# Attention scores from high and low parts in a one-core decoder trunk

## The chip, the cores and the metric

The kernel runs on one core of one Trainium2 chip. Its time is the device time of one launch in microseconds (us). The host lays the weights out in the order of their loads beforehand; that is not part of the time.

## The reference

One residual layer with stick-breaking attention, between two RMS norms; 256 rows, width 4096, 32 heads of 128.

```python
h = x + attn_branch(rms_norm(x, norm_attn), w_in_attn, w_out_attn)
out = rms_norm(h, final_norm)

# attn_branch: one product with a 4096 x 16384 matrix, the heads, one with a 4096 x 4096 matrix
q, k, v, g = split(xn @ w_in, 4)
z = q @ k.T / sqrt(128)                       # the scores of a head, 256 x 256, causal
log_fail = where(causal, log_sigmoid(-z), 0)
suffix = reverse_cumsum(log_fail) - log_fail
a = where(causal, exp(log_sigmoid(z) + suffix), 0)
branch = ((a @ v) * silu(g)) @ w_out
```

All data is float32.

## The kernel before

**The two large products.** Weights come in tiles `raw` of 128 rows by 2 x 512 numbers. Each is taken apart into a high part `wh` (a cast by ScalarE, ACT, to the rounded type fp32r) and a low part `wl` (a subtraction on VectorE, DVE). The activations have been split in the same way (`sh`, `sl`, later `oh`, `ol`). `mm3` then makes one product as three matmuls: high by high, high by low, low by high, each of 512 columns. "Product" below means these three matmuls on TensorE (PE). The work goes in units of two heads' width: 16 for the first matrix (units 0 to 15), 8 for the second. A unit has 16 steps; most units do part of their steps with 7 products instead of 8, for which DVE makes sums of tiles (`raw<-raw,raw`) after a DMA issued by GpSimd (POOL) has added one block of a tile onto another in place.

**The heads.** While unit u+1 multiplies, the two heads of unit u pass through `head(u, i)`. It transposes q and k on PE into the PSUM bank `tr`, copies them to SBUF with ACT (`qkT`), and makes the scores `z`, which hold 384 columns: the 128 x 128 block of late keys and late queries, and the 128 x 256 block of early keys. Then come the logarithm of the failure probability (`f`, four ACT operations and one on DVE), its high and low part (`fh`, `fl`), the suffix sums as matmuls with a triangle of ones (`neg_tri`, fp32r operands, called the scan here), the weights `a`, and the product with v (`o`). The scores and the product with v are matmuls of plain fp32 operands. In lines 848 to 852:

```python
        def scores():
            kw = dict(stop=False, skip_group_check=True)
            nc.tensor.matmul(z[:, 0:P], qk[:, 1, P:S], qk[:, 0, P:S], start=True, **kw)
            nc.tensor.matmul(z[:, P:BW], qk[:, 1, 0:P], qk[:, 0, :], start=False, **kw)
```

followed by a bf16 matmul with `ident_b` that adds a large negative number where a key does not come before its query (`off`).

**What sets the order.** No order is written out. The class `Plan` plays the kernel through while it is built: each step asks for an engine with an estimated cost, the step with the earliest due time goes next, and the instructions are recorded in that order, which each engine then keeps. Rings model the buffers: `gh` has 4 places of SBUF that all stages of the heads share, `att` is the one PSUM bank of the heads, `wl` has 5 places, `raw` has 7. `nc.take` waits for a place, `nc.give` hands it back. Products always go in the same sequence; work of the heads is put between them when it is ready in the plan. All instructions are recorded by one helper, so the profile gives nearly every one the line L132, and one goes by the names of tiles.

Of the kernel before, what the change touches and what calls it, by code (L numbers as in the profile page):

```python
# [10 lines left out]
F32 = mybir.dt.float32  # L11
F32R = mybir.dt.float32r
# [7 lines left out]
P = 128  # L20
S = 256
# [31 lines left out]
ROWS = 4  # L53
# [47 lines left out]
def vector_ns(n):  # L101
    return 67 + 1.0417 * n


def scalar_ns(n):
    return 98 + n / 1.2


def tensor_ns(n):
    return 0.4167 * n + 8.5 if n > 128 else 109.0  # L110
# [138 lines left out]
def kernel(  # L249
# [10 lines left out]
    nc = Plan(tc)  # L260
# [3 lines left out]
    wp = ctx.enter_context(tc.tile_pool(name="weights", bufs=1))  # L264
# [10 lines left out]
    def minus(out_, full, part):  # L275
        nc.vector.tensor_tensor(out=out_, in0=full, in1=part.bitcast(F32), op=ALU.subtract)
# [34 lines left out]
    for g, (n, k) in enumerate(order):  # L311
        p = parts[n]
        b = p["u"], p["prods"][k][0]
# [12 lines left out]
    def soon(c=4.0):  # L326
        return nc.here + 1e3 * c


    def dve(emit, n, key=None, more=0, **kw):  # L330
        n = n if isinstance(n, tuple) else (n,)
        cost = sum(vector_ns(m) for m in n) + 122 * (len(n) - 1) + more
        return nc.work("vector", cost, emit, soon() if key is None else key, **kw)

    def act(emit, n, key=None, **kw):
        n = n if isinstance(n, tuple) else (n,)
        cost = sum(scalar_ns(m) for m in n) + 100 * (len(n) - 1)
        return nc.work("scalar", cost, emit, soon() if key is None else key, **kw)


    FULL_P, FULL_S = (P,) * 2, (W,) * 2
# [3 lines left out]
    def ten(emit, *n):  # L345
        def others():
            nonlocal since_others
            since_others = 0
            emit()

        return nc.work("tensor", 40 + sum(tensor_ns(m) for m in n), others, nc.here - 1e4, wait=400)
# [469 lines left out]
    BW = 3 * P  # L821
    not_before = off.broadcast_to([P, 2, P])

    def head(u, i):
        yield nc.take("att", "gh", sooner=True)
        tr = att.tile([P, 2, S], F32, tag="att", name=f"tr{u}_{i}")

        def turn():
            for k in range(2):
                for t in range(NT):  # L830
                    c = k * CW + i * P
                    nc.tensor.transpose(tr[:, k, t * P : (t + 1) * P], st["qk", u][:, t, c : c + P], ident)

        yield ten(turn, P, P, P, P)
        if i == HG - 1:
            nc.give("one")
        qk = wp.tile([P, 2, S], F32, tag="gh", name=f"qkT{u}_{i}", bufs=ROWS)
        yield act(lambda: nc.scalar.copy(qk, tr), 2 * S)
        nc.give("att")
        yield nc.take("att", sooner=True)  # L840
        bank = att.tile([P, W], F32, tag="att", name=f"z{u}_{i}")
        z, gT = bank[:, 0:BW], bank[:, BW:W]

        def turned(to, t):
            nc.tensor.transpose(to, st["gv", u][:, t, i * P : (i + 1) * P], ident)

        def scores():
            kw = dict(stop=False, skip_group_check=True)
            nc.tensor.matmul(z[:, 0:P], qk[:, 1, P:S], qk[:, 0, P:S], start=True, **kw)
            nc.tensor.matmul(z[:, P:BW], qk[:, 1, 0:P], qk[:, 0, :], start=False, **kw)  # L850
            diagonal = z[:, 0 : 2 * P].rearrange("p (a b) -> p a b", a=2)
            nc.tensor.matmul(diagonal, ident_b, not_before, start=False, **kw)

        yield ten(scores, *FULL_P, *FULL_S, 2 * P)
        nc.give("gh")
        yield nc.take("gh", sooner=True)

        f = wp.tile([P, BW], F32, tag="gh", name=f"f{u}_{i}", bufs=ROWS)

        def soft():  # L860
            nc.scalar.activation(f, z, AF.Abs, scale=scale)
            nc.scalar.activation(f, f, AF.Exp, scale=-1.0)
            nc.scalar.activation(f, f, AF.Ln, bias=1.0)
            nc.scalar.activation(f, f, AF.Copy, scale=1.0 / scale)

        yield act(soft, (BW,) * 4)
        yield dve(
            lambda: nc.vector.scalar_tensor_tensor(out=f, in0=z, scalar=0.0, in1=f, op0=ALU.max, op1=ALU.add), BW
        )
        yield nc.take("gh", "gh", sooner=True)  # L870
        fh, fl = (wp.tile([P, BW], F32R, tag="gh", name=f"f{k}{u}_{i}", bufs=ROWS) for k in "hl")
        yield act(lambda: nc.scalar.copy(fh, f), BW)
        yield dve(lambda: minus(fl, f, fh), BW)
        nc.give("gh")

        if i == 0:
            yield nc.until(("gate", u))

        def scan():
            kw = dict(start=False, skip_group_check=True)  # L880
            nc.tensor.matmul(z, neg_tri, fh, stop=False, **kw)
            nc.tensor.matmul(z, neg_tri, fl, stop=False, **kw)
            nc.tensor.matmul(z[:, 2 * P : BW], neg_one, fh[:, 0:P], stop=False, **kw)
            nc.tensor.matmul(z[:, 2 * P : BW], neg_one, fl[:, 0:P], stop=True, **kw)
            turned(gT, 0)

        yield ten(scan, BW, BW, P, P, P)
        nc.give("gh", "gh")
        if i == 0:
            yield nc.take("gh", sooner=True)  # L890
            st["o", u] = wp.tile([P, 4, P], F32, tag="gh", name=f"gated{u}", bufs=ROWS)
        gated = st["o", u][:, 2 * i : 2 * i + 2, :].rearrange("p a b -> p (a b)")
        yield nc.take("gh", sooner=True)
        a = wp.tile([P, BW], F32, tag="gh", name=f"a{u}_{i}", bufs=ROWS)


        def weights_of():
            nc.scalar.activation(a, z, AF.Relu, scale=-scale)
            nc.scalar.activation(a, a, AF.Exp, scale=-1.0)

        yield act(weights_of, (BW, BW))
        yield act(lambda: nc.scalar.copy(gated[:, 0:P], gT), P)
        nc.give("att")
        yield nc.take("att", sooner=True)
        bank2 = att.tile([P, BW], F32, tag="att", name=f"o{u}_{i}")
        o, gT2 = bank2[:, 0:S], bank2[:, S:BW]
        v = lambda t: st["gv", u][:, t, CW + i * P : CW + (i + 1) * P]

        def out_of_head():
            kw = dict(skip_group_check=True)  # L910
            nc.tensor.matmul(o, v(0), a[:, P:BW], start=True, stop=False, **kw)
            nc.tensor.matmul(o[:, P:S], v(1), a[:, 0:P], start=False, stop=True, **kw)
            turned(gT2, 1)

        yield ten(out_of_head, *FULL_P, *FULL_S, P)
        nc.give("gh")
        if i == HG - 1:
            nc.give("two")
        yield act(lambda: nc.scalar.copy(gated[:, P:S], gT2), P)
        yield dve(lambda: nc.vector.tensor_tensor(out=gated, in0=o, in1=gated, op=ALU.mult), S)  # L920
        nc.give("att")
# [3 lines left out]
    def heads(u):  # L925
        nc.start(gate(u))
        yield nc.until(("qk", u))
        for i in range(HG):
            yield from head(u, i)

        nc.tell(("heads", u))
        if u < NS - 1:
            spill[u] = dp.tile([P, 4, P], F32, name=f"spill{u}")
            yield moved(
                "gpsimd", lambda: nc.gpsimd.dma_start(spill[u], st["o", u]), [4 * P], soon(),
                after=lambda: (nc.give("gh"), nc.tell(("spilled", u))),
            )
# [396 lines left out]
```

## Time and profile before

| | before |
|---|---|
| median of three timed runs | 1700.52 us (1699.19 to 1701.03) |
| profiled execution, its own time | 1698.9 us |
| span in that profile | 1697.1 us |
| granted TensorE clock, mean | 0.997 |
| PE busy | 1680.2 us, 99% |
| DVE busy | 1602.0 us, 94% |
| ACT busy | 1206.7 us, 71% |
| POOL busy | 324.9 us, 19% |
| HBM | 242 GB/s over the span |

Busy time is the union of the spans of an engine's instructions. Matmuls are pipelined: one of 512 columns lasts 0.38 us in the profile and yet the next starts 0.22 us after it, so the spacing tells the cost and not the length. DVE's instructions overlap a little in the same way. "PEld" is the weight load of a matmul, which has a row of its own. In the timeline, "x4" after a row means four instructions in a row that were merged.

### The profile page before, as it was taken

What the parts mean: (1) busy time and instruction counts of PE and PEld (TensorE: products, weight loads), DVE (VectorE), ACT (ScalarE), POOL (GpSimd) and SP (SyncE); (2) the same over time, 40 slices, a digit from 0 to 9 for tenths busy, and PEclk for the clock granted to TensorE, in tenths of its full rate; (3) what the DMA queues carried; (4) which work ended last, traced back from release to release, by engine and by line L of the source; (5) the groups of instructions that cost most, each with busy time, mean ns of one, the idle gap of its engine ahead of it and who ended that gap; (6) DMA issues with size and microseconds to landing.
All of it is one profiled execution on the core that took longest, in us unless ns stands there. A gap on an engine that the chain in (4) does not pass through costs nothing.

```text
span 1697.1 us, 25128 instructions
## 1 busy us (share of the span) xinstructions
PE 1680.2 (99%) x7776; PEld 1417.4 (84%) x7776; DVE 1602.0 (94%) x2025; ACT 1206.7 (71%) x1665; POOL 324.9 (19%) x400
## 2 busy tenths in 40 slices
PE   9999999999999999999999999999999999999997
PEld 7888888888888888888888888888888888888885
DVE  8899999999999999999999999999999978999997
ACT  8986767676767676767676767676868775656654
POOL 0012222121222222222212121212122111212110
PEclk9999999999999999999999999999999999999998
DMA  9978888878787878797978797979797978888895
GB/s 343 332 197 247 232 247 222 252 217 253 215 256 212 256 212 266 199 272 196 276 201 269 198 268 196 272 198 269 204 264 210 300 230 266 245 245 256 246 304 185
DMA packets 248438, 412.77 MB, mean 243 GB/s; under 512 B 28016, under 2 KB 72560, under 8 KB 248304
## 3 DMA queue, kind: packets, MB, share of 16 engines
q1 hardware_dynamic: 194544, 354.24, 62.7%
q0 software_dynamic: 53472, 56.65, 20.0%
q8 instruction: 61, 1.00, 0.2%
q14 instruction: 73, 0.60, 0.1%
q10 hardware_dynamic: 288, 0.28, 0.1%
HBM read 402.93 MB, written 8.13 MB: 242 GB/s over the span
## 4 chain that ended last, share of the span: by engine, by line
PE 94%; DVE 3%; DMA 1%; issue 1%; ACT 1%; SPq 0%; DVEq 0%; ACTq 0%
PE acc L132 89%; PE z L132 3%; PE o L132 1%; DVE wl L132 1%; PE tr L132 1%; DVE h L132 1%; DVE raw L132 0%; ACT wh L132 0%; DMA raw<-in_w_out_dram 0%; DMA raw<-in_w_in_dram 0%; DMA xres<-in_x_dram 0%; SPq L132 0%; ACT sq L132 0%; DVE scalars L132 0%; DVE qk_sb L132 0%
## 5 line engine op out<-in xcount | busy, mean ns | idle before, releaser
L132 ACT CAST wh<-raw 128x1024 fp32r<-128x1024 f32 (+1 forms) x989 | 919.3, 970 | 385.5 <-DVE raw L132 160.9
L132 DVE TENSOR_TENSOR wl<-raw,wh 128x1024 fp32r<-128x1024 f32 (+1 forms) x815 | 975.7, 1220 | 49.3 <-ACT wh L132 23.9
L132 PE MATMUL acc<-wh,sh 128*128 128x512 f32 x2048 | 771.9, 389 | 0.1
L132 PE MATMUL acc<-wh,sl 128*128 128x512 f32 x1898 | 727.1, 383 | 1.8 <-DVE sl L132 1.8
L132 PE MATMUL acc<-wl,sh 128*128 128x512 f32 x1748 | 668.9, 383 | 0.1
L132 PEld LDWEIGHTS acc<-wh,sh 128*128 128x128 f32 x2048 | 384.0, 188 | 77.9 <-DVE qk_sb L132 4.9
L132 POOL DMA_DIRECT2D raw<-in_w_in_dram x300 | 258.3, 947 | 972.2 <-DMA raw<-in_w_in_dram 375.1
L132 PEld LDWEIGHTS acc<-wh,sl 128*128 128x128 f32 x1898 | 356.0, 188 | 66.3 <-DVE sl L132 2.4
L132 PEld LDWEIGHTS acc<-wl,sh 128*128 128x128 f32 x1748 | 328.4, 188 | 55.6 <-DVE wl L132 0.4
L132 DVE TENSOR_TENSOR raw<-raw,raw 128x512 f32<-128x512 f32 x348 | 238.3, 688 | 15.3 <-DMA raw<-in_w_in_dram 11.7
L132 PE MATMUL acc<-wh,oh 128*128 128x512 f32 x512 | 192.4, 383 | 0.0
L132 PE MATMUL acc<-wh,ol 128*128 128x512 f32 x488 | 186.7, 383 | 0.0
L132 PE MATMUL acc<-wl,oh 128*128 128x512 f32 x464 | 177.6, 383 | 1.4 <-DVE wl L132 1.4
L132 DVE TENSOR_TENSOR wh<-raw,wh 128x512 fp32r<-128x512 f32 x174 | 119.7, 688 | 3.3 <-ACT wh L132 2.7
L132 DVE TENSOR_TENSOR raw<-raw 128x512 f32<-128x512 f32 x174 | 119.4, 686 | 0.0
L132 PEld LDWEIGHTS acc<-wh,oh 128*128 128x128 f32 x512 | 96.1, 188 | 17.3
L132 PEld LDWEIGHTS acc<-wh,ol 128*128 128x128 f32 x488 | 91.5, 188 | 16.1
L132 PEld LDWEIGHTS acc<-wl,oh 128*128 128x128 f32 x464 | 87.1, 188 | 17.6 <-DVE wl L132 2.2
L132 POOL DMA_DIRECT2D raw<-in_w_out_dram x48 | 41.5, 984 | 173.8 <-DMA raw<-in_w_out_dram 85.2
L132 ACT ACTIVATE f<-f 128x384 f32<-128x384 f32 x96 | 50.5, 526 | 3.0
L132 POOL DMA_DIRECT2D p<-spill x27 | 17.0, 676 | 89.9 <-DVE ol L132 32.0
L132 DVE SCALAR_TENSOR_TENSOR gv_sb<-acc,scalars,gv_sb 128x512 f32<-128x512 f32 x45 | 33.5, 745 | 0.0
(86 smaller groups left out, 765.7 us busy)
## 6 DMA issues: line engine op xcount, KB each, us to landing
raw<-in_w_in_dram SPq DMA_DIRECT2D x1024, 256.0 KB, 4.5
raw<-in_w_out_dram SPq DMA_DIRECT2D x256, 256.0 KB, 4.5
raw<-in_w_in_dram POOLq DMA_DIRECT2D x300, 128.0 KB, 5.2
p<-spill POOLq DMA_DIRECT2D x27, 256.0 KB, 4.6
raw<-in_w_out_dram POOLq DMA_DIRECT2D x48, 128.0 KB, 5.4
xr<-in_x_dram SPq DMA_DIRECT2D x16, 256.0 KB, 5.3
xres<-in_x_dram SPq DMA_DIRECT2D x16, 256.0 KB, 5.5
out_dram<-h SPq DMA_DIRECT2D x16, 256.0 KB, 2.8
```

The lines of the kernel that those rows point to most:

```text
L132: return self.tc.keep_in_program_order(getattr(self.engine, name)(*args, **kw))
```

## The change

`head` now makes two tiles out of the transposed q and k: `qkh`, which ACT writes rounded to fp32r, and `qkl`, which DVE writes as the difference between the PSUM bank and `qkh`. So the head takes a second place of the ring `gh` from here to the scores, and gives the PSUM bank back only after the subtraction. The two fp32 matmuls of the scores become six matmuls of fp32r operands, three for each block. The cost that the plan is told for the scores changes too.

```diff
-        qk = wp.tile([P, 2, S], F32, tag="gh", name=f"qkT{u}_{i}", bufs=ROWS)
+        yield nc.take("gh", sooner=True)
+        qk, ql = (wp.tile([P, 2, S], F32R, tag="gh", name=f"qk{k}{u}_{i}", bufs=ROWS) for k in "hl")
         yield act(lambda: nc.scalar.copy(qk, tr), 2 * S)
+        yield dve(lambda: minus(ql, tr, qk), 2 * S)
         nc.give("att")
...
-            nc.tensor.matmul(z[:, 0:P], qk[:, 1, P:S], qk[:, 0, P:S], start=True, **kw)
-            nc.tensor.matmul(z[:, P:BW], qk[:, 1, 0:P], qk[:, 0, :], start=False, **kw)
+            for keys, queries, to in ((slice(P, S), slice(P, S), z[:, 0:P]), (slice(0, P), slice(0, S), z[:, P:BW])):
+                for a, b in ((qk, qk), (qk, ql), (ql, qk)):
+                    first_ = a is b and keys.start == P
+                    nc.tensor.matmul(to, a[:, 1, keys], b[:, 0, queries], start=first_, **kw)
...
-        yield ten(scores, *FULL_P, *FULL_S, 2 * P)
-        nc.give("gh")
+        yield ten(scores, BW, BW, BW, 2 * P)
+        nc.give("gh", "gh")
```

Since the plan decides the order, instructions move. Three places of unit 5 show it; its first head is `5_0`, its second `5_1`, the number behind a tile's name is its buffer, and the number in `wl300` counts the split tiles.

On PE, the scores of head 5_0, before:

```order
L132 MATMUL acc6_5_5138<-wl293_5054,sh0_79 128x4x16x8
L132 MATMUL acc6_5_5138<-wh293_5017,sl0_80 128x4x16x8
L132 MATMUL z5_0_5148<-qkT5_0_5136 128x128
L132 MATMUL z5_0_5148<-qkT5_0_5136 128x256
L132 LDWEIGHTS ident_b_140
L132 MATMUL z5_0_5148<-off_139,ident_b_140 128x256
L132 MATMUL acc6_3_5157<-wh293_5017,sh0_79 128x4x32x4
```

and now:

```order
L132 MATMUL acc6_3_5214<-wh293_5077,sl0_80 128x4x16x8
L132 MATMUL z5_0_5221<-qkh5_0_5196 128x128
L132 MATMUL z5_0_5221<-qkl5_0_5197,qkh5_0_5196 128x128
L132 MATMUL z5_0_5221<-qkh5_0_5196,qkl5_0_5197 128x128
L132 MATMUL z5_0_5221<-qkh5_0_5196 128x256
L132 MATMUL z5_0_5221<-qkl5_0_5197,qkh5_0_5196 128x256
L132 MATMUL z5_0_5221<-qkh5_0_5196,qkl5_0_5197 128x256
L132 LDWEIGHTS ident_b_140
L132 MATMUL z5_0_5221<-off_139,ident_b_140 128x256
L132 MATMUL acc6_1_5233<-wh294_5106,sh1_86 128x4x32x4
```

Six matmuls stand where two stood (the profile shows each of the two fp32 ones as two). Counted in the whole order, the scores of a unit's first head stand 5 products after its transposes where 3 stood between; for the second head it is 5 in both, and its transposes and scores stand one product earlier than they did. The scan of the first head stays at its product and that of the second moves one product earlier; the product with v stays where it was. Only in unit 15, whose heads run beside the first products with the second matrix, is the shift larger: its first scores stand 14 products after the transposes instead of 2, and its last product with v 15 products later than before.

On DVE, the stretch behind the last addition that makes q, k, v and g of unit 5 (`gv_sb5<-acc5_3`), before:

```order
L132 SCALAR_TENSOR_TENSOR gv_sb5_5027<-acc5_3_4356,scalars_77,gv_sb5_5027 128x512
L132 TENSOR_TENSOR wl297_5144<-raw97_0_4990,wh297_5068 128x1024
L132 TENSOR_TENSOR raw98_0_5019<-raw98_0_5019,raw98_1_5006 128x2x256
L132 TENSOR_TENSOR raw98_1_5006<-raw98_0_5019,raw98_1_5006 128x2x256
L132 TENSOR_TENSOR raw98_0_5019<-raw98_0_5019 128x2x256
L132 SCALAR_TENSOR_TENSOR f5_0_5163<-z5_0_5148,f5_0_5163 128x384
L132 TENSOR_TENSOR wl300_5200<-raw98_1_5006,wh300_5112 128x1024
L132 SCALAR_TENSOR_TENSOR gl5_5158<-gv_sb5_5027,gl5_5158 128x512
L132 TENSOR_TENSOR fl5_0_5197<-f5_0_5163,fh5_0_5196 128x384
L132 TENSOR_TENSOR wl301_5223<-raw98_0_5019,wh301_5142 128x1024
L132 TENSOR_TENSOR wl304_5233<-raw100_0_5150,wh304_5211 128x1024
L132 TENSOR_TENSOR wl302_5243<-raw99_0_5034,wh302_5180 128x1024
```

and now:

```order
L132 SCALAR_TENSOR_TENSOR gv_sb5_5087<-acc5_3_4401,scalars_77,gv_sb5_5087 128x512
L132 TENSOR_TENSOR qkl5_0_5197<-tr5_0_5182,qkh5_0_5196 128x512
L132 TENSOR_TENSOR wl297_5205<-raw97_0_5050,wh297_5128 128x1024
L132 TENSOR_TENSOR raw98_0_5079<-raw98_0_5079,raw98_1_5066 128x2x256
L132 SCALAR_TENSOR_TENSOR gl5_5215<-gv_sb5_5087,gl5_5215 128x512
L132 TENSOR_TENSOR raw98_1_5066<-raw98_0_5079,raw98_1_5066 128x2x256
L132 TENSOR_TENSOR wl302_5254<-raw99_0_5094,wh302_5235 128x1024
L132 TENSOR_TENSOR raw98_0_5079<-raw98_0_5079 128x2x256
L132 SCALAR_TENSOR_TENSOR f5_0_5244<-z5_0_5221,f5_0_5244 128x384
L132 TENSOR_TENSOR gv_sb5_5087<-gv_sb5_5087,gl5_5215 128x2x256
L132 TENSOR_TENSOR wl300_5287<-raw98_1_5066,wh300_5172 128x1024
L132 TENSOR_TENSOR wl301_5299<-raw98_0_5079,wh301_5203 128x1024
```

The new subtraction stands in front of `wl297`. The gate (`gl5`, `gv_sb5<-gv_sb5,gl5`) and `wl302` have moved ahead of `wl300`; `fl5_0` has moved back, behind `wl304`.

On DVE, behind the scores of head 5_1, where it makes the sums of tile pairs 103 and 104, before:

```order
L132 TENSOR_TENSOR wl318_5443<-raw104_0_5368,wh318_5434 128x1024
L132 TENSOR_TENSOR fl5_1_5437<-f5_1_5401,fh5_1_5436 128x384
L132 TENSOR_TENSOR raw103_1_5259<-raw103_0_5329,raw103_1_5259 128x2x256
L132 TENSOR_TENSOR raw103_0_5329<-raw103_0_5329 128x2x256
L132 TENSOR_TENSOR raw104_0_5368<-raw104_0_5368,raw104_1_5348 128x2x256
L132 TENSOR_TENSOR wl316_5475<-raw103_1_5259,wh316_5392 128x1024
L132 TENSOR_TENSOR wl317_5483<-raw103_0_5329,wh317_5419 128x1024
```

and now:

```order
L132 TENSOR_TENSOR fl5_1_5509<-f5_1_5464,fh5_1_5508 128x384
L132 TENSOR_TENSOR wl318_5515<-raw104_0_5432,wh318_5505 128x1024
L132 TENSOR_TENSOR raw103_1_5316<-raw103_0_5395,raw103_1_5316 128x2x256
L132 TENSOR_TENSOR raw104_0_5432<-raw104_0_5432,raw104_1_5413 128x2x256
L132 TENSOR_TENSOR raw103_0_5395<-raw103_0_5395 128x2x256
L132 TENSOR_TENSOR wl316_5549<-raw103_1_5316,wh316_5470 128x1024
L132 TENSOR_TENSOR raw104_1_5413<-raw104_0_5432,raw104_1_5413 128x2x256
L132 TENSOR_TENSOR wl317_5566<-raw103_0_5395,wh317_5488 128x1024
```

The first sum of pair 104, which needs the block that POOL's DMA adds, has moved ahead of the last sum of pair 103.

## The prediction

> **What bounds the kernel now.** I read the page first: the busy times, then the chain that ended last.
>
> ```profile
> PE   1680.2 (99%) x7776; PEld 1417.4 (84%) x7776; DVE 1602.0 (94%) x2025; ACT 1206.7 (71%) x1665; POOL 324.9 (19%) x400
> PE 94%; DVE 3%; DMA 1%; issue 1%; ACT 1%; SPq 0%; DVEq 0%; ACTq 0%
> ```
>
> TensorE is hardly ever idle, and 94% of the chain is its work. DVE is a close second, so both have to be priced. The changed work lies where heads run. I took the sums over the fourteen regular units of that stretch (28 of the 32 heads), then the waits of the matrix engine's loads and of DVE there.
>
> ```profile
> core 0: us, PE busy (x) PEld busy (x) DVE busy (x) ACT busy (x) POOL busy (x), PEclk, DMA share, GB/s
> 178.00:1355.00 1177.00, 1176.91 (x5490) 994.05 (x5488) 1135.65 (x1361) 856.06 (x1139) 247.13 (x294) 1.00 0.83 236
> ```
>
> ```profile
> PEld acc L132 <- DVE qk_sb L132: 4.9, 14, 0.5
> PEld acc L132 <- PE acc L132: 4.7, 14, 0.3
> ```
>
> ```profile
> DVE wl L132 <- ACT wh L132: 13.6, 18, 0.9
> DVE raw L132 <- DMA raw<-in_w_in_dram: 11.7, 10, 2.1
> DVE wl L132 <- PE acc L132: 4.9, 17, 0.3
> DVE wl L132 <- ACT qk_sb L132: 3.7, 11, 0.3
> ```
>
> PE is busy for 1176.91 of 1177 us at full clock. The only wait of its loads on DVE is 0.35 us once per unit, at the unit's start (a bank handed back by `qk_sb`); no product waits for a low part `wl`. DVE is idle for 1177 - 1135.65 = 41.3 us, 3.0 us per unit. The third DVE row matters: 17 times DVE waits for PE to free a place of `wl`, so it regularly runs as far ahead as the ring allows.
>
> So time here is PE's sequence. An edit costs what it adds to that sequence, or what it makes PE wait.
>
> **The scores on PE.** The transposes and the scores of head 5_0, from the timeline (start, length):
>
> ```profile
> 515.30 0.60 PE L132 MATMUL tr<-ident,qk_sb 128*128 128x128 f32 x4
> 515.65 0.47 PE L132 MATMUL acc<-wh,sh 128*128 128x512 f32 x1
> ...
> 517.74 0.40 PE L132 MATMUL acc<-wh,sl 128*128 128x512 f32 x1
> 517.97 0.82 PE L132 MATMUL z<-qkT 128*128 128x128 f32 x4
> 518.63 0.27 PE L132 MATMUL z<-off,ident_b 128*128 128x256 bf16 x1
> 518.66 0.47 PE L132 MATMUL acc<-wh,sh 128*128 128x512 f32 x1
> ```
>
> From end to end, the four fp32 passes take 517.97 + 0.82 - (517.74 + 0.40) = 0.65 us. What comes behind them does not change. The price of the new form is read from the scan of the same head, whose operands are fp32r already:
>
> ```profile
> 529.84 0.38 PE L132 MATMUL acc<-wh,sl 128*128 128x512 f32 x1
> 530.07 0.34 PE L132 MATMUL z<-fh,neg_tri 128*128 128x384 f32 x1
> 530.24 0.33 PE L132 MATMUL z<-fl,neg_tri 128*128 128x384 f32 x1
> 530.41 0.22 PE L132 MATMUL z<-fh,neg_tri 128*128 128x128 f32 x1
> 530.47 0.28 PE L132 MATMUL z<-fl,neg_tri 128*128 128x128 f32 x1
> ```
>
> The ends are 530.57, 530.63 and 530.75. The first matmul of 128 columns adds 0.06 us, since its weights were loaded under the 384 columns ahead of it. The second adds 0.12: 128 columns stream in 0.055 (512 go in 0.22), so it waited for its load, which takes 0.11 to 0.12. Now the six: the first adds 0.06 (loaded under a product), the next two wait for loads, 0.11 to 0.12 each; the fourth waits 0.05 to 0.06 more for its load and streams 256 columns in 0.11, so 0.17; the fifth and sixth stream 0.11 under loads of 0.11 to 0.12. The sum is 0.06 + 0.23 + 0.17 + 0.23, about 0.67 to 0.69 us. I take 0.67, near the lower end, because the four transposes, each behind a load of its own, follow each other every 0.11 us ((0.60 - 0.27) / 3, the last one's length taken as that of the mask, 0.27). That is 0.02 us more than now, and 32 heads give **+0.6 us**. The ends are 0.50 us if all loads hid (3 x 0.055 + 3 x 0.11), which is -0.15 x 32 = -5 us, and 0.71 us with every load at 0.12, +2 us.
>
> ```profile
> L132 PEld LDWEIGHTS z<-qkT x128: 186/191/193, 95.5 to 1385.9; 128*128 128x128 f32 x128
> L132 PEld LDWEIGHTS z<-fh,neg_tri x64: 186/188/189, 104.3 to 1398.5; 128*128 128x128 f32 x64
> ```
>
> A load of fp32r weights lasts 188 ns and one of fp32 weights 191, so nothing shows that the new type loads faster. The Trainium skill ("TensorE: Matmul & The Clock Gate", section "Weight-path perf modes") says that a fast weight load is on for 128 weight columns of any type but FP32. Were fp32r such a type, all loads would hide and the sum would be 5 us less; these two rows speak against it.
>
> **The subtraction on DVE.** It reads 512 columns from PSUM. The nearest row is an addition of that shape from PSUM; how long it holds the queue is read from the spacing of two 512-column operations.
>
> ```profile
> L132 DVE TENSOR_TENSOR gv_sb<-acc,gv_sb 128x512 f32<-128x512 f32 x28 | 19.2, 685 | 0.0
> ```
>
> ```profile
> 547.58 0.55 DVE L132 TENSOR_TENSOR fl<-f,fh 128x384 fp32r<-128x384 f32 x1
> 548.05 0.69 DVE L132 TENSOR_TENSOR raw<-raw,raw 128x512 f32<-128x512 f32 x1
> 548.65 0.69 DVE L132 TENSOR_TENSOR raw<-raw 128x512 f32<-128x512 f32 x1
> 551.47 0.69 DVE L132 TENSOR_TENSOR raw<-raw,raw 128x512 f32<-128x512 f32 x1 [2.13 <-DMA raw<-in_w_in_dram]
> ```
>
> It lasts 0.69 and holds the queue for 0.60 us: 19.2 us over 32 heads, 16.8 in the fourteen units, 1.2 per unit of 3.0 idle. I cost it at nothing, covered by that idle time, if the idle time stands where it can be used. That is checked at the two places of the order.
>
> First place, behind `gv_sb5<-acc5_3`:
>
> ```profile
> 517.42 0.75 DVE L132 SCALAR_TENSOR_TENSOR gv_sb<-acc,scalars,gv_sb 128x512 f32<-128x512 f32 x1
> 518.09 1.22 DVE L132 TENSOR_TENSOR wl<-raw,wh 128x1024 fp32r<-128x1024 f32 x1
> 519.22 1.42 DVE L132 TENSOR_TENSOR raw<-raw,raw 128x512 f32<-128x512 f32 x2
> 522.59 1.23 DVE L132 TENSOR_TENSOR wl<-raw,wh 128x1024 fp32r<-128x1024 f32 x1 [0.89 <-ACT wh L132]
> ```
>
> ```profile
> 516.76 0.58 ACT L132 COPY qkT<-tr 128x512 f32<-128x512 f32 x1
> ...
> 526.98 0.38 PE L132 MATMUL acc<-wl,sh 128*128 128x512 f32 x1
> ...
> 557.11 0.38 PE L132 MATMUL acc<-wl,sh 128*128 128x512 f32 x1
> ```
>
> ACT's copy (now a cast, about as long) ends at 517.34, so `qkl` can start when `gv_sb` leaves the queue, at 518.09, and ends at 518.78. The scores come five products after the transposes: 515.65 + 0.09 (the first row there is longer than 0.38 by that) + 5 x 0.66 = 519.04. So the new wait ends 0.26 us ahead of PE, and the first matmul of the six does not even read `qkl`. Then, by the new order and spacings of 0.60 (512 columns), 1.13 (1024) and 0.47 (384): `wl297` 518.69, sum 519.82, `gl` 520.42, sum 521.02, `wl302` 521.62, sum 522.75, `f` 523.35, gate 523.82, `wl300` 524.42, done 525.65. Its first reader on PE is the row at 526.98 (counted in the order), 1.3 us later. Before, this `wl300` started at 522.59 after an idle 0.89 us in which DVE waited for ACT, busy with the head; that hole is filled now, with `wl302`. `wl301`, `wl304`, `wh305` and `fl` follow and end by about 529.0; the scan that reads `fl` starts at 530.07. Nothing is late, by 1 us.
>
> Second place: DVE waits 2.13 us for the block that POOL adds to tile pair 104. That DMA doesn't depend on the heads, so `qkl5_1`, which stands before this hole, shrinks it to about 1.5. But the last sum of pair 103 now queues behind the wait: it starts at 552.07 instead of 548.65, ACT casts its result by 553.8, and DVE makes `wl317` from 554.4 to 555.6 instead of from 553.2 (551.47 + 0.60 + 1.13). PE reads it at 557.11, 1.5 us later. Held up, not late. If the slot for that DMA came free 0.6 us later, SP's load and POOL's add would be 0.6 later too, still inside the 1.5.
>
> **The rest.**
>
> ```profile
> L132 ACT COPY qkT<-tr 128x512 f32<-128x512 f32 x32 | 18.6, 581 | 1.0 <-PE tr L132 1.0
> L132 ACT CAST wh<-raw 128x512 fp32r<-128x512 f32 x176 | 108.3, 616 | 78.1 <-PE acc L132 59.6 <-DMA raw<-in_w_in_dram 8.8 <-DMA raw<-in_w_out_dram 7.7
> ```
>
> ACT writes fp32r where it copied: 0 to 35 ns more by these rows, 1 us in all, on an engine idle for 27% of the stretch. The bank `tr` is held until `qkl` ends; its next taker is the same head's `z`, priced above. The second place in `gh` is taken ahead of others' requests; in regular units it is given back long before the head's widest moment. In unit 15 it isn't free at once: those scores stand 14 products after the transposes, and the last product with v 15 products later. The block that needs it is the last step of the next unit, 32 products or 21 us on, so I cost this at nothing; if the cover is gone, a few us.
>
> **Sum.** 1698.9 (the profiled execution) + 0.6 = 1699.5. The median of the timed runs, 1700.52, lies 1.6 above that execution, so I forecast 1700.5 + 0.6 = **1701.1 us**. Runs spread over 1.8 us, so 0.2% (3.4 us) is about what a measurement can tell from no change.
>
> **Rivals.**
> *DVE becomes the bound (slower).* For: idle time that waits for ACT or a DMA may move along with the work instead of being filled; only the waits for PE, 4.9 us, are sure to give way. Then the fourteen units pay 16.8 - 4.9 = 12 us, about 1713 with the 0.6. It decides where DVE reaches `qkl` more than 0.26 us late: from there each delay is PE's own, since matmuls keep their order. Partial forms, 0.3 us at each head, give +10. Against: the hole of 0.89 us is one that the new order demonstrably fills. Chance 0.28.
> *Loads hide and the six matmuls stream (faster).* 0.50 instead of 0.65 us, 32 heads, -5 us: 1695.5. For: the fp32 form streams two columns' time per column and pass, so four passes' worth against three. The Trainium skill ("FP8 and Floating Point Precision", section "TensorE Precision Notes") lists true FP32 as four passes, H*H, H*L, L*H and L*L; three products leave out the last. Against: the 0.12 us of the scan's last fp32r matmul. Chance 0.11.
> *My forecast,* nothing but the small PE term: 0.61.
>
> **Numbers.** The range leaves out the strongest form of each rival: from 1697.0 (most of the -5 less measurement scatter) to 1710.0 (most of the +10). Faster by over 0.2%: 0.11; within: 0.61; slower: 0.28.
>
> **What would show it.** Right: the six score matmuls and the mask take 0.02 us more than before from end to end; DVE busy up by about 22 us as rows (0.69 each); its idle time in the fourteen units down to some 24 us; no waits of PE on `qkl` or `wl`. Wrong: a row "z <- DVE qkl" among PE's waits with more than 0.1 us per head, or products waiting for `wl`; or score matmuls of 128 columns that follow each other at 0.055 us.

## The result, and the profile after

| | before | after |
|---|---|---|
| median of nine runs each, same chip | 1699.38 us (1697.87 to 1701.03) | 1704.64 us (1703.80 to 1705.96) |
| ratio to before, 95% interval | | 1.0031 [1.0022, 1.0040] |
| profiled execution, its own time; span | 1698.9; 1697.1 us | 1705.03; 1703.3 us |

The change made the kernel 5.3 us slower. That is inside the range, but not the likeliest case (1701.1); it lies on the side that was given 0.28.

The page of the changed kernel, first the busy times, then the shares of the chain that ended last:

```profile
PE   1685.2 (99%) x7840; PEld 1419.7 (83%) x7840; DVE 1624.7 (95%) x2057; ACT 1203.1 (71%) x1665; POOL 325.4 (19%) x400
PE 86%; DVE 9%; issue 3%; DMA 1%; ACT 1%; SPq 0%; DVEq 0%; ACTq 0%
```

DVE's rows grew by 22.7 us, as priced, and the chain now goes through DVE for 9% instead of 3%. The fourteen regular units, with busy time and count of each engine:

```profile
178.00:1355.00 1177.00, 1175.60 (x5518) 991.05 (x5517) 1150.04 (x1381) 847.38 (x1132) 247.09 (x293) 1.00 0.83 234
```

DVE is still idle for 27 us there (41.3 before). PE idles for 1.4 us by this count, but the union of overlapping matmuls hides short gaps; the waits of the weight loads show them (total us, times, longest):

```profile
PEld acc L132 <- DVE gv_sb L132: 7.4, 14, 0.5
PEld acc L132 <- PE acc L132: 4.7, 14, 0.4
PEld acc L132 <- DVE qk_sb L132: 4.7, 14, 0.3
```

The last two rows were there before. The first is new: 14 times, once per unit, 0.5 us. It names neither `qkl` nor `wl` but a bank: products wait until DVE has added up the bank that they are to write. And DVE is not short of time; among its own waits in the same stretch, the one for PE has grown from 4.9 to 12.5 us and the one for a DMA (11.7 us) is gone:

```profile
DVE wl L132 <- PE acc L132: 12.5, 26, 0.7
DVE wl L132 <- ACT qk_sb L132: 4.8, 14, 0.4
DVE wl L132 <- ACT wh L132: 0.9, 5, 0.3
```

The place, again in unit 5. First PE (start, length): transposes, two of the rows in front of the wait and behind it, and the first of the scores:

```profile
517.21 0.60 PE L132 MATMUL tr<-ident,qk_sb 128*128 128x128 f32 x4
...
519.41 0.39 PE L132 MATMUL acc<-wl,sh 128*128 128x512 f32 x1
519.64 0.39 PE L132 MATMUL acc<-wh,sl 128*128 128x512 f32 x1
520.12 0.49 PE L132 MATMUL acc<-wh,sh 128*128 128x512 f32 x1
520.45 0.39 PE L132 MATMUL acc<-wl,sh 128*128 128x512 f32 x1
...
521.40 0.40 PE L132 MATMUL acc<-wh,sl 128*128 128x512 f32 x1
521.64 0.23 PE L132 MATMUL z<-qkh 128*128 128x128 f32 x1
```

the weight load of the matmul at 520.12, with the idle time before it and what ended it:

```profile
520.12 0.19 PEld L132 LDWEIGHTS acc<-wh,sh 128*128 128x128 f32 x1 [0.52 <-DVE gv_sb L132]
```

and DVE at the same time:

```profile
517.53 0.75 DVE L132 SCALAR_TENSOR_TENSOR gv_sb<-acc,scalars,gv_sb 128x512 f32<-128x512 f32 x1
518.19 1.22 DVE L132 TENSOR_TENSOR wl<-raw,wh 128x1024 fp32r<-128x1024 f32 x1
519.32 0.74 DVE L132 SCALAR_TENSOR_TENSOR gv_sb<-acc,scalars,gv_sb 128x512 f32<-128x512 f32 x1
519.99 0.68 DVE L132 TENSOR_TENSOR qkl<-tr,qkh 128x512 fp32r<-128x512 f32 x1
```

The two products in front of the scores, from 520.12 on, are those that open bank 3 for the next unit (`acc6_3`). DVE hands that bank back with `gv_sb5<-acc5_3`, which ends at 519.32 + 0.74 = 520.06. Without a wait the first matmul would have started 0.22 after 519.64, at 519.86. It starts at 520.12, 0.26 us late, and because no load had run ahead the next one follows after 0.33 instead of 0.22: 0.37 us in all.

DVE is no later than it was: its addition ends 520.06 - 517.21 = 2.85 us after the start of the transposes, and 517.42 + 0.75 - 515.30 = 2.87 before. PE is earlier at bank 3. Before, the scores stood in front of `acc6_3`, which started 518.66 - 515.30 = 3.36 us after the transposes; without them in between PE would be there after 2.65. The scores and their mask had been the cover for the hand-back.

The other part is the six matmuls themselves, here of head 5_1, where no such wait stands:

```profile
542.78 0.38 PE L132 MATMUL acc<-wh,sl 128*128 128x512 f32 x1
543.00 0.22 PE L132 MATMUL z<-qkh 128*128 128x128 f32 x1
543.06 0.28 PE L132 MATMUL z<-qkl,qkh 128*128 128x128 f32 x1
543.17 0.27 PE L132 MATMUL z<-qkh,qkl 128*128 128x128 f32 x1
543.28 0.33 PE L132 MATMUL z<-qkh 128*128 128x256 f32 x1
543.45 0.28 PE L132 MATMUL z<-qkl,qkh 128*128 128x256 f32 x1
543.57 0.28 PE L132 MATMUL z<-qkh,qkl 128*128 128x256 f32 x1
543.69 0.28 PE L132 MATMUL z<-off,ident_b 128*128 128x256 bf16 x1
543.73 0.47 PE L132 MATMUL acc<-wh,sh 128*128 128x512 f32 x1
```

From the end at 543.16 to the end at 543.85 they take 0.69 us (0.65 before); from the first score matmul to the next product it is 0.73 us (518.66 - 517.97 = 0.69 before).

The sum over a unit, from the distances between the starts of consecutive matmuls in units 2 to 13: 84.07 us before, 84.52 after. Of the 0.45, 0.353 lie between products and 0.091 in the scores and scans. Times 14 that is 4.9 + 1.3 = 6.2 us, all that the span grew by (1703.3 - 1697.1). From unit 15's first transposes to the end it is 342 us in both.

### The profile page after: what moved, and what is told of

It reads as the page before. It is cut to its first block, busy times and chain, and to the rows that moved or that the text cites. A ratio compares the mean times of both kernels' runs of the same rounds, so it can differ in the third digit from the quotient of the medians.

```text
span 1703.3 us, 25320 instructions
## 1 busy us (share of the span) xinstructions
PE 1685.2 (99%) x7840; PEld 1419.7 (83%) x7840; DVE 1624.7 (95%) x2057; ACT 1203.1 (71%) x1665; POOL 325.4 (19%) x400
## 4 chain that ended last, share of the span: by engine, by line
PE 86%; DVE 9%; issue 3%; DMA 1%; ACT 1%; SPq 0%; DVEq 0%; ACTq 0%
PE acc L132 82%; PE z L132 3%; DVE gv_sb L132 2%; DVE wl L132 2%; DVE raw L132 2%; PE o L132 1%; DVE qk_sb L132 1%; DVE h L132 1%; PE tr L132 0%; DMA raw<-in_w_out_dram 0%; ACT wh L132 0%; DMA raw<-in_w_in_dram 0%; DMA xres<-in_x_dram 0%; SPq L132 0%; DVE wh L132 0%
```

## The experiments

Theory A: the loss is the hand-back of bank 3, which PE reaches too early since the scores moved behind its products; the rest is the six matmuls. Theory B: it is the subtraction's 0.6 us per head on a DVE that is 94% busy, whatever the order. All ratios are to the kernel before on the same chip.

**1. Only the scores moved.** The kernel before, with its fp32 scores and no subtraction; the plan holds the scores of a unit's first head back for 1500 ns instead of 400, so that they stand behind both products with bank 3.

```diff
-    def ten(emit, *n):
+    def ten(emit, *n, wait=400):
...
-        yield ten(scores, *FULL_P, *FULL_S, 2 * P)
+        yield ten(scores, *FULL_P, *FULL_S, 2 * P, wait=400 if i else 1500)
```

> The kernel before, with one number changed: the first head of each unit asks for its scores 1.1 us later in the plan, so that in the order they stand five products after the transposes, as in the changed kernel, behind the two products that open the bank of gv_sb<-acc_3. The scores stay fp32 and there is no subtraction. Theory A (the order: PE reaches that bank before DVE has handed it back, because the scores no longer stand in front of it): 0.27 us in each of 15 units, +4 us against before, and in the profile about 0.5 us of waiting per unit of the weight loads for DVE gv_sb. Theory B (the load on DVE: the subtraction makes everything behind it later): 0 us, since DVE has no more to do.

Measured: 1704.43 us against 1698.55, ratio 1.0034 [1.0021, 1.0048]. That is 5.9 us where 4 were expected: the expectation counted only the 0.27 us of a wait, and at 0.37 us each fifteen units give 5.6. Its waits of the loads in the fourteen units:

```profile
PEld acc L132 <- DVE gv_sb L132: 7.4, 14, 0.5
PEld acc L132 <- DVE qk_sb L132: 4.7, 14, 0.3
PEld acc L132 <- PE acc L132: 4.7, 14, 0.3
```

The new wait is there to the tenth, with neither of the things that the change is made of. In this order the second head has moved too: its scores stand 2 products behind its transposes instead of 5. But the only new wait is the one at bank 3, as in the changed kernel, so the later place of the first head's scores is enough to make the loss.

**2. Only six matmuls.** The kernel before with ACT writing fp32r and each block of the scores made three times from the high parts; the low parts are left out.

```diff
+            for keys, queries, to in ((slice(P, S), slice(P, S), z[:, 0:P]), (slice(0, P), slice(0, S), z[:, P:BW])):
+                for k in range(3):
+                    nc.tensor.matmul(to, qk[:, 1, keys], qk[:, 0, queries], start=k == 0 and keys.start == P, **kw)
```

> The kernel before, with q and k cast to fp32r and each block of the scores made by three matmuls of that one tile (high by high, three times). The low parts are left out, so the scores are three times the rounded ones. Nothing is added on DVE and the scores stay where they stood. Both theories: only the price of six fp32r matmuls against two fp32 ones, 0.047 us x 32 = +1.5 us. If the order mattered for nothing, all of the +5.3 us would have to show here or in the next run.

Measured: 1698.86 us, ratio 1.0001 [0.9992, 1.0010]: 0.3 us, with 1.5 just inside the interval. In its trace the scores and scans of a unit take 0.093 us longer, as in the changed kernel, and the products 0.025 less. So the price of the six is some 0.3 to 1.5 us and explains only the small part of the loss.

**3. Only the subtraction.** The kernel before with one more subtraction of 512 columns per head on DVE, which nobody reads, in line behind the scores.

```diff
+        yield nc.take("gh", sooner=True)
+        ql = wp.tile([P, 2, S], F32R, tag="gh", name=f"qkl{u}_{i}", bufs=ROWS)
+        yield dve(lambda: minus(ql, qk, qk), 2 * S)
```

> The kernel before, with a subtraction of 512 columns added on DVE to each head, behind the scores; its result is read by nobody. The scores stay fp32 and stand where they stood on PE. Theory A: 0 us, within 1 us. Theory B: +4 us or more, most of the +5.3 us.

Measured: 1697.15 us, ratio 0.9992 [0.9983, 1.0000]: 1.4 us less than before, where a change within 1 us was expected. The fourteen units and the waits of its loads there:

```profile
178.00:1355.00 1177.00, 1176.66 (x5501) 996.27 (x5500) 1156.51 (x1392) 856.71 (x1142) 247.97 (x294) 1.00 0.83 237
```

```profile
PEld acc L132 <- PE acc L132: 2.4, 7, 0.4
PEld acc L132 <- DVE qk_sb L132: 2.0, 6, 0.3
```

DVE is busy for 1156.51 us, more than in the changed kernel, and PE waits less than before: the plan, told of one more step, has put DVE's work in an order in which half of the units lose their two old waits. By the distances between matmuls each of the two waits costs about 0.2 us, which makes 0.2 us per unit on the average when half of the units lose both. The mean of units 2 to 13 is 0.19 us shorter, so no cost of the load is left to see. Theory B, that the load costs whatever the order, is out. This subtraction does not stand where the changed kernel has it, and nobody waits for it; the next run has it in its place.

**4. The changed kernel, bank 3 first.** Bank 5 is added up twice, then bank 3 once. The plan lets other work in after each of these steps, unless it is told not to hold; with bank 5's second addition not holding, bank 3's (`gv_sb<-acc_3`) stands ahead of `wl296` instead of behind it.

```diff
-                yield add_scaled(two[:, t, :], 5, two[:, t, :], 3, t)
+                yield add_scaled(two[:, t, :], 5, two[:, t, :], 3, t, hold=t == 1 or u >= OUT0)
```

> The changed kernel, with the additions out of bank 5 not holding up the one out of bank 3 in the plan: on DVE gv_sb<-acc_3 moves ahead of one wl, 1.13 us earlier. PE's order stays as in the changed kernel. Theory A: the wait for the bank goes, 0.27 us in each of 15 units: 4 us less than the changed kernel, +1.5 us against before. Theory B: no change, +5.3 us against before.

Measured: 1699.01 us, ratio 1.0002 [0.9993, 1.0011], 0.5 us above before where 1.5 were expected; the loss is gone, and so is the row:

```profile
PEld acc L132 <- PE acc L132: 4.8, 14, 0.4
PEld acc L132 <- DVE qk_sb L132: 4.7, 14, 0.3
```

All parts of the change are in it. In PE's order the first head's scores even stand 6 products behind the transposes instead of 5, still behind both products with bank 3. The hand-back of bank 3 is now the second half of this DVE row:

```profile
515.15 0.60 PE L132 MATMUL tr<-ident,qk_sb 128*128 128x128 f32 x4
515.48 1.60 DVE L132 SCALAR_TENSOR_TENSOR gv_sb<-acc,scalars,gv_sb 128x512 f32<-128x512 f32 x2
```

It ends 515.48 + 1.60 - 515.15 = 1.93 us after the start of the transposes, before PE is there at about 2.65; in the changed kernel it was 2.85. One addition that stands one instruction sooner is worth nearly the whole difference (5.3 us less 0.5, each against the kernel before on its own chip).

**5. The kernel before with the same edit**, as a control.

> Control: the kernel before with the edit that mended the changed kernel (bank 3's addition on DVE ahead of the low part, wl296). Theory A: in the kernel before PE never waited for bank 3, since the scores stood in front of its products, so the edit has nothing to take away: within 1 us of before, 1697.6 to 1699.6. If the edit is worth 4 us or more here as well, it mends something of its own and says nothing on the change.

Measured: 1699.03 us, ratio 1.0001 [0.9992, 1.0010]: the edit gains nothing where there was no wait for bank 3, as Theory A says. It is not a clean control, since the plan moved the heads too: the first scores stand 4 products behind the transposes instead of 3, so the first product with bank 3 now comes ahead of them, and the second head comes 7 products sooner. With the earlier hand-back that makes no wait for bank 3.

**6. All three hand-backs in a row, kernel before.** Both additions of bank 5 not holding, so the three stand together.

```diff
-                yield add_scaled(two[:, t, :], 5, two[:, t, :], 3, t)
+                yield add_scaled(two[:, t, :], 5, two[:, t, :], 3, t, hold=u >= OUT0)
```

> The kernel before (fp32 scores where they were), with both additions of bank 5 no longer held back in the plan: on DVE the two hand-backs of bank 5 and that of bank 3 then run one behind the other, ahead of the subtraction that makes the low part wl296. Theory A (the loss is bank 3 handed back too late for a PE that arrives without the scores in front of it; hand-backs of banks are what PE waits for at the head of a unit): the two old waits of PE's loads there, 0.35 us each in 14 units, shrink or go; the one on 'acc by PE' (4.7 us in 14 rows) should go, that on qk_sb (4.9 us) stays: 14 x 0.33 = 4.7, so 4 to 5 us less than before, 1694 to 1695. Theory B (DVE's load is what costs; order on DVE only moves the wait to the low parts): the low parts come 1.2 us later, PE waits for them, and the time is the same or up to 5 us above before.

Measured: 1694.26 us against 1699.05, ratio 0.9974 [0.9963, 0.9984]: the fastest version, faster than both kernels. The old wait at bank 5 is gone (the second row, 0.2 us once, was not among the waits of before):

```profile
PEld acc L132 <- DVE qk_sb L132: 4.5, 13, 0.4
PEld tr L132 <- DVE gated L132: 0.2, 1, 0.2
```

Not all of the gain is that wait. Between the profiled spans (1697.1 us before, 1691.4 here), 3.5 us lie in units 1 to 13 and 1.7 us from unit 14 on; here too the heads have moved in PE's order, the second one 7 products forward.

**7. The same edit on the changed kernel.**

> The changed kernel (three products, scores behind five products) with the same edit: both additions of bank 5 and that of bank 3 one behind the other on DVE. Theory A: no row 'acc by DVE gv_sb' among the waits of PE's loads; 1704.6 less 5.6 (the wait on bank 3, as in the run that put bank 3's addition ahead of the low part), less up to 4.7 if the wait at bank 5 goes too: 1694.5 to 1699. If it is 0.3 to 1.5 us above the same edit on the kernel before, what is left of the change is the six matmuls alone. Theory B: DVE carries 19 us more here than in the kernel before with the same edit, so this one is 5 us or more above that one.

Measured: 1699.00 us (1697.19 to 1703.39), ratio 1.0005 [0.9997, 1.0014]: nothing gained over run 4, and 4.7 us above run 6. The regular unit is 83.9 us, 0.11 more than in run 6, which makes 1.5; one longer wait stands at the start of unit 15, and it is for the hand-back `gv_sb` again:

```profile
1356.86 0.46 PE L132 MATMUL acc<-wh,oh 128*128 128x512 f32 x1 [1.34 <-DVE gv_sb L132]
```

In PE's order the first scores stand 4 products behind the transposes here, not the 5 that the expectation names. Being 4.7 us above run 6 comes close to what Theory B forecast (5 us or more). But between the two profiled spans (1691.4 and 1697.1 us) only 1.4 us lie in units 1 to 13, where DVE carries most of the added work, and 0.09 of the 0.11 us per unit lie in the scores themselves. From unit 14 on it is 3.8 us, of which the wait above makes 1.5. So the next pair left unit 15 alone.

**8 and 9. The same, but not in unit 15**, which is treated as in run 4 (`hold=u >= OUT0 - t`) or as in the changed kernel (`hold=u >= OUT0 - 1`).

> The changed kernel with the three hand-backs one behind the other in units 0 to 14 only; in unit 15, whose hand-backs meet the start of the second matrix, as in the run that only put bank 3's addition ahead of the low part. That both additions moved gave 1699.0 on the changed kernel, 4.7 above the same edit on the kernel before, though its regular units have only 0.11 us more each (1.5 in all). If the rest was lost at unit 15 (one wait of 1.7 us there), this kernel comes to 1694.3 + 1.5 = 1695.8 to 1697.5 and its profile lacks that wait. If the rest is spread, or is a cost of the subtraction on DVE (Theory B), it stays at 1698.5 to 1699.5.

> The same, with unit 15's hand-backs left as they are in the changed kernel. If what was lost lies at unit 15, this is 0.5 to 1 us above the other kernel of this pair (a wait of 0.6 us for bank 3 in unit 15 that the changed kernel has), 1696.3 to 1698. If it is spread, 1698.5 to 1699.5.

Measured: 1699.33 us (1697.74 to 1703.03), 1.0006 [0.9997, 1.0014], and 1699.79 us (1698.09 to 1706.35), 1.0006 [0.9997, 1.0015]. Neither gains on run 7, and the long wait at the start of unit 15 is in both of their profiles too. But the pair did not try what it was meant to try. This is DVE in unit 15, in run 6 and then in run 7:

```profile
1350.20 2.25 DVE L132 SCALAR_TENSOR_TENSOR gv_sb<-acc,scalars,gv_sb 128x512 f32<-128x512 f32 x3
```

```profile
1353.52 1.40 DVE L132 SCALAR_TENSOR_TENSOR gv_sb<-acc,scalars,gv_sb 128x512 f32<-128x512 f32 x2
1354.84 1.22 DVE L132 TENSOR_TENSOR wl<-raw,wh 128x1024 fp32r<-128x1024 f32 x1
1355.97 0.75 DVE L132 SCALAR_TENSOR_TENSOR gv_sb<-acc,scalars,gv_sb 128x512 f32<-128x512 f32 x1
```

Run 6 has the three hand-backs in a row. In run 7 the plan put a `wl` of 1.22 us ahead of bank 3's hand-back in spite of the edit, and in runs 8 and 9 one stands there as well. So whether the loss at unit 15 hangs on the order there was not tried and stays open.

DVE's waits in the fourteen units suggest why the times scatter. Run 6, then run 7, then run 9 (whose profiled execution was one of 1706.35 us):

```profile
DVE wl L132 <- PE acc L132: 11.6, 26, 0.5
```

```profile
DVE raw L132 <- DMA raw<-in_w_in_dram: 5.0, 7, 1.2
DVE wl L132 <- issue: 1.7, 11, 0.2
DVE wl L132 <- PE acc L132: 0.8, 5, 0.2
```

```profile
DVE raw L132 <- DMA raw<-in_w_in_dram: 14.4, 12, 2.4
DVE wl L132 <- ACT wh L132: 7.4, 19, 0.9
DVE wl L132 <- issue: 0.6, 4, 0.2
DVE wl L132 <- PE acc L132: 0.2, 1, 0.2
```

In run 6 DVE waits 26 times for PE to free a low part's place: it has run as far ahead as it may. In runs 7 and 9 this wait is nearly gone. A faster PE and 19 us more work seem to have used up DVE's lead, so its waits for DMAs come through. In run 7's profile that costs PE nothing there yet (its loads wait 4.9 us for `qk_sb`, as in the kernel before); in run 9's profile they wait 9.7 us for it at the heads of units:

```profile
PEld acc L132 <- DVE qk_sb L132: 9.7, 14, 1.9
```

With PE's waits for the banks mended, DVE does become late in some executions, and the times scatter over 5 to 8 us instead of 2 to 5. That is a reading of waits in single profiles. What makes the rest of the 4.7 us was not measured and stays open.

## Why the prediction was right or wrong

- **The time:** 1704.64 us lies inside the range of 1697.0 to 1710.0 by luck. The range was drawn wide for the rivals; the sum itself said +0.6 us, and the +5.3 us comes mainly from a wait that neither the sum nor a rival names.
- **PE's sequence sets the time:** held. All of the 6.2 us of span is found in distances between matmuls.
- **The scores on PE:** the sum gave 0.67 to 0.69, and it is 0.69; I took the lower end. With the mask behind them the block is 0.04 to 0.05 us longer instead of 0.02, 1.3 us over the fourteen units instead of 0.6 over all. Loads do not hide (128-column matmuls follow at 0.11, not 0.055), so the faster rival fell. The Trainium skill ("TensorE: Matmul & The Clock Gate", section "LDWEIGHTS (loading the stationary operand)") puts a load at its columns divided by 1.2, in ns, which gives an estimate of 107 for 128 columns; the spacing of 0.11 us agrees with that, while a load's own row in the profile lasts 188 to 191 ns. The four passes for true FP32 that the Trainium skill lists ("FP8 and Floating Point Precision", section "TensorE Precision Notes"), and on which the rival drew, promise no gain here: four fp32 passes took 0.65 us, and the six matmuls, at the pace of such loads, 0.69.
- **The subtraction on DVE at nothing:** right for this kernel. Run 3 shows it for the added work alone, and run 4 with the subtraction in its place. Its readers were on time: no wait on `qkl` or `wl`. Idle time in the units fell to 27 us where 24 were said.
- **First place, "Nothing is late, by 1 us":** the step that failed. It followed each DVE instruction behind `gv_sb5<-acc5_3` to its reader and never asked who waits for that instruction itself. Moving the scores was treated as free ("What comes behind them does not change"), though the quoted order shows `acc6_3` behind the scores before, and in front of them now. The rows were at hand: the hand-back ends at 517.42 + 0.75 = 518.17, and PE without the scores in front is there at 517.97. That is 0.2 us late, with 0.11 for the load that does not run ahead 0.3, and 4.3 us over fourteen units. With 0.6 for the matmuls this would have made +4.9 us; +5.3 was measured.
- **Second place, "Held up, not late":** held; the DMA wait there is not shrunk to 1.5 us but gone from the list.
- **Unit 15 and ACT at nothing:** held, 342 us from unit 15 to the end in both (a new wait of 0.9 us for `gv_sb` at its start is made up for).
- **Rival "DVE becomes the bound":** gave the right side with the wrong mechanism. In the changed kernel DVE waits for PE more than before; the subtraction stands behind the late hand-back and does not delay it. It came near to being true only in run 9's profile, once PE no longer waited for the banks.

## What to carry to other kernels

When a block of work moves in an in-order queue, price both sides: not only whether it is ready at its new place, but what it had covered at the old one. For each instruction that moves up, write down when its inputs and its output bank come free beside when the engine will now reach it. And where one engine waits at the same point of every unit for a buffer's hand-back, the order on the engine that hands back can be worth more than its load: here one addition ahead of a subtraction was worth 4.8 us, while in run 3 some 19 us of added work on that engine cost nothing. And where an order is made by a plan, look at what else an edit has moved: most of the edits here moved the heads on PE too, and in unit 15 those of runs 7 to 9 did not make the order that they were meant to make.

## What the runs showed of the hardware

- A gap in a stream of matmuls costs more than the wait: the load that carried the wait did not run under the matmul ahead of it (it started at 520.12, together with its own matmul), and the next matmul followed after 0.33 us instead of 0.22. A wait of 0.26 us thus cost 0.37.
- Busy time did not show the loss: PE's share stayed at 99%, and its union fell by only 1.3 us in the fourteen units while 4.9 us were lost between products.
